# Chosen key blocks of the samples: turned by VectorE in 32x32 blocks and scored in sixteen 32x32 tiles, with the values as a stream of their own

## The chip, the cores and the metric

The kernel runs on one core of a Trainium2 chip, as one launch. The metric is the device time of that launch in microseconds (us). TensorE (PE in the profile; PEld is its weight load), VectorE (DVE), ScalarE (ACT), GpSimd (POOL) and SyncE (SP) each take their own instructions in the order in which they were written, and meet at semaphores. SP issues nearly all transfers.

## What is computed

One inference step of one hybrid layer: a prompt of 256 tokens and a sample group of 8 sequences with 8 new tokens each, and 2048 past tokens a sequence in paged caches. All data are 32-bit floats. Cut to what matters here:

```
u = RMSNorm(x) @ w_in                        # 2048 -> 23664 columns, split among the mixers
y = x + (sigmoid(m_A) * (GDN(u) @ w_branch_a) + sigmoid(m_B) * (NSA(u) @ w_branch_b)) @ w_out
# NSA, for a sample sequence, 16 heads in 4 groups, head dim 128: three attentions are summed
#   compressed keys -> importance -> the chosen blocks of 64 keys (13 best of 30, and 3 always kept)
#   chosen:  s = q @ k.T * 128 ** -0.5 + bias;  p = softmax(s over chosen keys);  o = p @ v
#   window:  the same over the last 512 past tokens
# GDN: a gated delta rule with a state of 128 x 128 a head
```

For the chosen blocks the kernel scores all 2048 past keys of a sequence (16 pages of 128 tokens x 4 groups x 128, 256 KB a page, fetched by page number) and adds a mask m that is very low for a block that was not chosen. Queries of a sequence are 4 groups x 32 rows (4 heads x 8 tokens), so scores and outputs use the 128 partitions as four quarters of 32, one a group.

## The kernel before

The program is written by Python streams (generators). Class `Run` keeps a rough clock of every engine while it writes the program; it always lets that stream take its next step which can start first by this clock. What comes out is a fixed order of instructions on each engine. All compute calls go through the helper at L320 (transfers through L292), so the profile is read by tile names, not by lines.

The backbone is the projection stream: weights are loaded to `wraw` (tiles of 1 MB, three of them), split by ACT into a rounded part `whi` and by DVE (some by POOL) into a rest `wlo` (pieces of 128x512), at most four pieces ahead of TensorE, and multiplied as three matmuls of 320 columns a 128x128 block into `acc` (`acc<-hhi,whi`, `acc<-hlo,whi`, `acc<-hhi,wlo`). It has the lowest claim on TensorE and so fills what other streams leave. Its slabs are queued in stages: until the samples' attention is done, the queue holds only the slabs of queries, keys, values, gates and of 16 heads' z_A, 4752 projection matmuls in all; the slabs of the delta net are queued by code that stands behind `run.go(lambda: done["sample"] == 3)`.

In the samples' part three things come one after the other and overlap: compressed keys (`compressed`, pages `cpg`), window (`window`), chosen blocks (`sample`). `sample` is run twice at the same time (`worker(0)`, `worker(1)`), each for four sequences with ten page tiles `spg` of its own, first the 16 key pages of a sequence and then its 16 value pages. For keys (`scores`, two pages at a time) each page is turned on TensorE by four 128x128 transposes into PSUM (`nt`), copied to SBUF (`kT`, DVE and ACT in turn), and multiplied by the queries:

```
for g in range(4):
    T.transpose(nt[:, g * P:g * P + P], pg[:, g * P:g * P + P], ident)
...
for g in range(4):
    T.matmul(ns[32 * g:32 * g + 32, (p - e.nt + k) * P:(p - e.nt + k + 1) * P], qT(b, g), kT[:, g * P:g * P + P], start=True, stop=True)
```

Each of these score products contracts over 128 rows and fills 32 output rows. Four pages share a bank `ns`, which DVE scales and masks into `xs` (128 x 2112). Then come the 64 new keys, the maximum (DVE), the exponential (ACT), and `weighted`: probabilities `xs` are transposed on TensorE four pages at a time (`nt`), copied (`pT`) and multiplied with the value pages (`op`). The result `o` is turned once more (`tp`) and kept in `obS`, which goes to memory as `d_ob` at the end of all eight.

Behind this stage stands the gated delta net, 16 groups, in which DVE is the busiest engine beside TensorE, and the branch and output products.

Of the kernel before, what the change touches and what calls it, by code (L numbers as in the profile page):

```python
# [21 lines left out]
P = 128  # L22
DM = 2048
NT = 320                 # token columns: 256 of the prompt, then 8 x 8 of the samples
TP = 256
B = 8
# [8 lines left out]
NV = 647                 # distances 519..-127, falling  # L35
NU = 383                 # distances -127..255, rising
WC = 2048                # words a partition of a tile of weights
NRC = 3                  # tiles of weights loaded
NHI = 4                  # pieces of weights split ahead
NPL = 4                  # the first pieces, all split by Pool  # L40
NLP = 4                  # one of so many pieces is split by Pool
CR = -1                  # rank of the compressed keys
OR = -4                  # rank of the moving operand of branch B
NWP = 5                  # pages of the window loaded ahead
SW = ((10, (0, 1, 2, 4)), (10, (3, 5, 6, 7)))  # two streams of chosen blocks: pages loaded ahead, sequences
NM = 3                   # slabs of gates made at the end of the delta net
ZS = (0, 1, 2, 4, 6, 8, 10, 12, 14, 16, 18, 20, 22, 24, 26, 28)  # heads whose z_A are made before the delta net starts


# ---------------------------------------------------------------- constants of the shapes alone  # L50
# [31 lines left out]
def _packs():  # L82
# [48 lines left out]
    tok = np.flatnonzero(i % 32 < 16)                      # of the samples: sequences g and g + 4 at 32 g, their queries 16 behind  # L131
# [26 lines left out]
def bc(ap, dims):  # L158
    """The same memory with other free dimensions [step, count]."""
    return bass.AP(tensor=ap.tensor, offset=ap.offset, ap=[list(ap.ap[0])] + [list(x) for x in dims])  # L160
# [9 lines left out]
class Clock:  # L170
    """A rough clock of every engine, kept while the program is emitted, to order the streams of work by."""
    # from the end of an engine's instruction to the start of one that waits for it
# [4 lines left out]
    def __init__(self):  # L177
        self.t = dict.fromkeys(("pe", "act", "dve", "pool", "sp", "dge", "dma"), 0.0)
        self.parts, self.cut, self.psum = {}, {}, set()          # cut: of a bank: the column that parts it in two
        self.slot = {}                                     # of a tile's name: its place in its pool  # L180
        self.w, self.r = {}, {}                            # of a place: (time, engine) of its last write, read
        self.last = (0.0, "sp")
        self.set, self.lock, self.narrow, self.cold = None, False, False, True

    def key(self, ap):
        n = ap.tensor.name
        k = self.slot.get(n)
        if k is None:                                      # an input or output: nothing waits for it
            return None
# [49 lines left out]
    def table(self, name):  # L239
        """The functions that ACT is loaded with."""  # L240
# [27 lines left out]
class Timed:  # L268
    """An engine whose instructions also move the clock."""
# [4 lines left out]
    def __getattr__(self, op):  # L274
# [9 lines left out]
        def g(*a, **k):  # L284
# [8 lines left out]
            if self.name == "pe":  # L293
# [12 lines left out]
                if self.clock.cold:                        # TensorE at half its speed  # L306
                    ns *= 2
# [16 lines left out]
class Run:  # L324
    """Emits several streams of work, always the one whose next step can start first by the clock.

    A stream yields, before each step, the engine that the step starts on, alone or with the tiles that it waits for
    (alone: it waits for the result of its last step), or a function that is true once the stream may go on."""
# [18 lines left out]
    def _start(self, x):  # L347
# [9 lines left out]
        if e == "exp":                                     # on ACT, with the functions of EXPSET  # L357
# [24 lines left out]
class Next:  # L382
    """The place that the next tile of a tag will have."""
# [12 lines left out]
class Place(Next):  # L396
    """A part of a tile that is written again."""
# [8 lines left out]
class Pool:  # L406
    """A pool of tiles that tells the clock which tiles share a place."""
# [18 lines left out]
def step(ctx: ExitStack, tc: tile.TileContext, I, O):  # L426
# [25 lines left out]
    def newton(y, x, t):  # L452
        """One step of y towards x ** -0.5."""
# [54 lines left out]
    def pieces():  # L508
        """Conditions to wait for, then pieces of weights, in the order of their products."""
# [73 lines left out]
    # ------------------------------------------------------------ normalised input  # L583
# [30 lines left out]
    def gain():  # L614
        """The gain on every partition."""
# [31 lines left out]
    def x_turn(ti, xt, ss, q):  # L647
        """Four columns of tiles of the input, normalised, turned and in two parts."""
# [28 lines left out]
    # ------------------------------------------------------------ tables of the relative bias  # L677
    lastB = tab.tile([P, 520], F32, name="lastB")              # of the last 512 past tokens and the 8 new ones
    winB = tab.tile([P, 8], F32, name="winB")                  # of the first of them, out of the window
# [3 lines left out]
    pB = btab.tile([P, 16, 256], F32, name="pB")               # columns rise with the distance  # L683
# [71 lines left out]
    # ------------------------------------------------------------ native sparse attention  # L755
# [72 lines left out]
    def rstd(pl, pp, tag, src, n, exact, tags=("sq", "rs", "nt")):  # L828
        """(mean of squares over the partitions + eps) ** -0.5 on every partition; a generator."""
# [44 lines left out]
    def prepare():  # L874
        # b, a and the gates by token
# [111 lines left out]
    def prompt():  # L987
        yield lambda: done["names"]
        qp = {}
        for g, tt in ((g, tt) for g in range(4) for tt in range(2)):  # L990
# [8 lines left out]
            # compressed keys, the four heads of the group at once  # L999
# [79 lines left out]
    # ---- samples: compressed keys  # L1079
# [11 lines left out]
    class Feed:  # L1091
        """Tiles loaded ahead of their use, in order."""
# [6 lines left out]
        def load(self):  # L1099
            for r in self.reqs:  # L1100
# [3 lines left out]
                self.out.append(r(t))                      # what is to be written once it is there  # L1104
# [17 lines left out]
    def page(key, b, p):  # L1122
        def f(t):
            k = key[2:], b
            if k not in pnum:                              # the page numbers of a sequence, for its keys and values
                for x in [x for x in pnum if x[0] == k[0] and x[1] % 2 == b % 2 and k[0] == "sel" or x[0] == k[0] == "cmp"]:
                    del pnum[x]
# [99 lines left out]
    def select(h):  # L1227
        """The 13 best of the blocks 1..30 (lower index first among equals); 0, 31 and 32 are always kept."""
# [32 lines left out]
    # ---- samples: window  # L1261
    class Env:
        """Where a stream of attention of the samples keeps its tiles: PSUM tags of sums and transposes, pool and number of others."""
# [17 lines left out]
    def scores(e, b, npg, dst, kS, finish):  # L1281
        """Raw products of the queries of b with npg pages of keys and the 64 new keys."""
# [94 lines left out]
    def add_o(x, g, b):  # L1377
        """Into the sum over the branches."""
# [16 lines left out]
    # ---- samples: chosen blocks  # L1395
    sm = pool(nsa_ctx, "sm")
    obS = sm.tile([P, 16, 64], F32, name="obS")

    def sample(smp, sps, n, bs):
        req = [page(key, b, p) for b in bs for key in ("k_sel", "v_sel") for p in range(16)]  # L1400
        env = Env(sps, "s", "t", 2, smp, 2, "", Feed(smp, "spg", n, req))
        for b in bs:
# [924 lines left out]
```

## Time and profile before

| | |
|---|---|
| time, median of 3 runs | 2684.83 us (2684.65 to 2687.64) |
| profiled execution: span on the core | 2682.3 us; the page gives no other time of it, and the median run lies 2.5 us above this span |
| TensorE busy | 97% of the span |
| DVE, ACT, POOL busy | 63%, 51%, 25% |
| chosen blocks | from about 822 to 1172 us of the span |
| transfers in that stretch | 292 GB/s, 0.86 of the 16 DMA engines' time |

A record of the profile is one hardware instruction. A matmul of 32-bit operands other than the transposes and the projection's (whose operands are rounded parts) shows as two weight loads and two matmuls, two passes. Records overlap on TensorE, since a matmul starts before the one ahead has drained, so what one costs is read from the distance between starts and not from its own length.

### The profile page before, as it was taken

The numbers are of one execution on the slowest core, as the hardware profiler recorded it, in microseconds if no ns is written. First come the engines' busy times: TensorE is split into PE (matmuls) and PEld (weight loads), VectorE is DVE, ScalarE is ACT, GpSimd is POOL, SyncE is SP. The second block draws the span as 40 slices with busy tenths as digits, with TensorE's granted clock in tenths as the row PEclk, the third lists the DMA queues.
The fourth block names the chain that finished last, engine by engine and source line by source line (L and its number), as shares of the span: only waits on it lengthen the run. The fifth ranks groups of instructions, "written<-read, shape, count | busy, mean of one in ns | idle before, by whom it ended". The sixth has DMA issues, their size and how long they took to land.

```text
span 2682.3 us, 58837 instructions
## 1 busy us (share of the span) xinstructions
PE 2612.6 (97%) x22228; PEld 2330.2 (87%) x22228; DVE 1701.1 (63%) x3738; ACT 1358.9 (51%) x3098; POOL 675.2 (25%) x913
## 2 busy tenths in 40 slices
PE   7999999999999999999999999999999999999999
PEld 6898888887888888899889898888888879999999
DVE  5554446555554655445987888888888875455543
ACT  5453443344343333336667666666666555544443
POOL 2000011000000000012454554555545444211111
PEclk9999999999999999999999999999999989999999
DMA  6747776878768898865345455444454355756554
GB/s 198 235 143 254 240 246 214 271 263 281 255 231 307 284 336 286 283 210 179 117 146 163 154 157 177 135 138 147 138 167 156 129 184 185 228 179 193 179 190 133
DMA packets 548671, 543.84 MB, mean 203 GB/s; under 512 B 32482, under 2 KB 452499, under 8 KB 548003
## 3 DMA queue, kind: packets, MB, share of 16 engines
q1 hardware_dynamic: 534308, 493.67, 57.1%
q0 software_dynamic: 14080, 46.41, 5.0%
q8 instruction: 175, 2.87, 0.4%
q14 instruction: 108, 0.88, 0.1%
HBM read 470.31 MB, written 69.67 MB: 201 GB/s over the span
## 4 chain that ended last, share of the span: by engine, by line
PE 86%; DVE 10%; issue 2%; ACT 1%; DMA 0%; POOL 0%; SPq 0%; DVEq 0%; ACTq 0%; POOLq 0%
PE acc L320 61%; PE ps L320 6%; PE nt L320 4%; PE op L320 3%; PE pp L320 3%; PE ns L320 2%; DVE wlo L320 2%; PE tp L320 1%; PE p L320 1%; DVE cv L320 1%; PE sp L320 1%; PE bank L320 1%; DVE at L320 1%; DVE Xd L320 1%; PE ms L320 1%
## 5 line engine op out<-in xcount | busy, mean ns | idle before, releaser
L320 PE MATMUL acc<-hhi,whi 128*128 128x320 f32 (+1 forms) x3472 | 1159.8, 334 | 1.2 <-ACT whi L320 0.8
L320 PE MATMUL acc<-hhi,wlo 128*128 128x320 f32 (+1 forms) x3472 | 1078.6, 311 | 1.1 <-DVE wlo L320 1.1
L320 PE MATMUL acc<-hlo,whi 128*128 128x320 f32 (+1 forms) x3472 | 1077.7, 310 | 0.4 <-DVE hlo L320 0.4
L320 ACT ACTIVATE whi<-wraw 128x512 fp32r<-128x512 f32 (+1 forms) x996 | 626.0, 630 | 866.9 <-PE acc L320 806.0
L320 DVE TENSOR_TENSOR wlo<-wraw,whi 128x512 fp32r<-128x512 f32 x838 | 606.7, 727 | 507.4 <-ACT whi L320 498.0
L320 PEld LDWEIGHTS acc<-hhi,whi 128*128 128x128 f32 (+1 forms) x3472 | 657.6, 189 | 93.4 <-issue 73.7
L320 PEld LDWEIGHTS acc<-hlo,whi 128*128 128x128 f32 (+1 forms) x3472 | 658.7, 190 | 7.6 <-issue 2.4
L320 PEld LDWEIGHTS acc<-hhi,wlo 128*128 128x128 f32 (+1 forms) x3472 | 656.8, 189 | 1.9 <-DVE wlo L320 1.9
L320 POOL TENSOR_TENSOR wlo<-wraw,whi 128x512 fp32r<-128x512 f32 (+1 forms) x158 | 208.8, 1322 | 420.6 <-ACT whi L320 389.3
L320 DVE SCALAR_TENSOR_TENSOR cv<-xp,cw,cv 128x344 f32<-128x344 f32 x192 | 139.6, 728 | 30.7 <-ACT cv L320 28.6
L292 POOL DMA_DIRECT2D d_mz<-raw x48 | 26.4, 550 | 523.8 <-ACT raw L320 489.1
L320 PE MATMUL acc<-oah,whi 128*128 128x320 f32 x512 | 158.2, 309 | 0.0
L320 PE MATMUL acc<-oal,whi 128*128 128x320 f32 x512 | 158.2, 309 | 0.0
L320 PE MATMUL acc<-oah,wlo 128*128 128x320 f32 x512 | 158.2, 309 | 0.0
L320 ACT ACTIVATE kT<-nt 128x512 f32<-128x512 f32 x80 | 47.7, 596 | 101.0 <-PE ns L320 55.2
L320 PEld LDWEIGHTS acc<-oah,whi 128*128 128x128 f32 x512 | 96.1, 188 | 0.0
L320 PEld LDWEIGHTS acc<-oal,whi 128*128 128x128 f32 x512 | 96.1, 188 | 0.0
L320 PEld LDWEIGHTS acc<-oah,wlo 128*128 128x128 f32 x512 | 96.1, 188 | 0.0
L320 DVE COPY kT<-nt 128x512 f32<-128x512 f32 x80 | 55.2, 691 | 63.9 <-PE ns L320 41.3
L320 POOL TENSOR_TENSOR vx<-v,pk_gdn 128x512 fp32r<-128x512 f32 x64 | 68.7, 1073 | 82.1 <-DVE v L320 39.7
L320 PE MATMUL pp<-cpg,Pk 128*32 128x512 f32 x608 | 82.7, 602 | 0.0
L320 POOL TENSOR_TENSOR sS<-sS,ends 128x1024 f32<-128x1024 f32 x32 | 61.8, 1930 | 38.8 <-PE ps L320 38.7
(422 smaller groups left out, 3613.8 us busy)
## 6 DMA issues: line engine op xcount, KB each, us to landing
wraw<-w_in SPq DMA_DIRECT2D x136, 1024.0 KB
wraw<-w_in SPq DMA_DIRECT2D x97, 512.0 KB
cpg<-cache_k_cmp SPq DMA_DIRECT2D x128, 256.0 KB
cpg<-cache_v_cmp SPq DMA_DIRECT2D x128, 256.0 KB
spg<-cache_k_sel SPq DMA_DIRECT2D x128, 256.0 KB
spg<-cache_v_sel SPq DMA_DIRECT2D x128, 256.0 KB
wraw<-w_branch_a SPq DMA_DIRECT2D x32, 1024.0 KB
sS<-state_gdn SPq DMA_DIRECT2D x32, 512.0 KB
```

Of the source, the lines that this page charges most:

```text
L292: return f(*a, **k)
L320: return f(*a, **k)
```

## The change

The two workers become three streams: `quarters`, `keys` and `values`.

- `quarters` copies the queries `qs` once into `q4` by 16 transfers from SBUF to SBUF: quarter d of the head dimension (32 rows) is put on each of the four quarters of the partitions.
- `keys` takes the sequences in order. It has six page tiles `spg` of its own. For each half of a sequence (8 pages) DVE turns every page in blocks of 32x32 straight from `spg` to `kT` (`V.transpose`, one instruction of 128x512 a page; no PSUM, no copy); `kT` holds 8 pages and has one place. Then TensorE multiplies 64 times: for each quarter d of the head dimension, each quarter k of the page's tokens and each group g, one product with 32 rows, 32 output rows and 256 columns (8 pages x 32 tokens); the four d are summed in PSUM, and the four k lie in four different banks `ns`. DVE merges the four banks into `xs` at the end of both halves, so the softmax follows as before. Keys of sequence b start once the values of b-2 are done.
- `values` is `weighted` unchanged, on ten page tiles `spv`, with one PSUM place for the transposed probabilities where there were two for each worker; it follows one sequence behind the keys, and starts once all compressed keys are done.

The page numbers of a sequence are read into registers once for its keys and once for its values, where one reading served both. The diff, cut to its core (the rest takes comments out):

```
-SW = ((10, (0, 1, 2, 4)), (10, (3, 5, 6, 7)))
+NKP, NVP = 6, 10
...
-            k = key[2:], b
+            k = key if key[2:] == "sel" else "cmp", b
...
-    def sample(smp, sps, n, bs):
-        req = [page(key, b, p) for b in bs for key in ("k_sel", "v_sel") for p in range(16)]
-        env = Env(sps, "s", "t", 2, smp, 2, "", Feed(smp, "spg", n, req))
-        for b in bs:
-            yield lambda: done["sel"] > b // 4
...
-            yield from scores(env, b, 16, xs, ksS, fin_s)
...
+    kfeed = Feed(smk, "spg", NKP, [page("k_sel", b, p) for b in range(B) for p in range(16)])
+    ready = []
...
+    def quarters():
...
+        for k in range(4):
+            for d in range(4):
+                yield ("sp", qs)
+                SY.dma_start(q4[32 * k:32 * k + 32, d], qs[32 * d:32 * d + 32])
...
+    def keys():
...
+        for b in range(B):
+            yield lambda: done["sel"] > b // 4 and done["sample"] >= b - 1
...
+            for half in range(2):
+                kT = smk.tile([P, 8, 512], F32, tag="kT", name="kT")
+                for i in range(8):
+                    pg = yield from kfeed.get()
+                    yield ("dve", pg, Place(clock, kT))
+                    V.transpose(kT[:, i], pg)
+                    kfeed.release()
+                yield ("pe", kT, q4, *ns)
+                for d in range(4):
+                    for k, rows in enumerate(quad):
+                        for g in range(4):
+                            T.matmul(ns[k][quad[g], 256 * half:256 * half + 256], q4[rows, d, b, 4 * g:4 * g + 4, :].rearrange("p h t -> p (h t)"),
+                                     kT[rows, :, P * g + 32 * d:P * g + 32 * d + 32], start=d == 0, stop=d == 3)
+            for k in range(4):
+                yield ("dve", ns[k])
+                V.scalar_tensor_tensor(bc(xs[:, 32 * k:], [[P, 16], [1, 32]]), ns[k].rearrange("p (a c) -> p a c", c=32), SCALE,
+                                       bc(m[:, k // 2:], [[2, 16], [0, 32]]), op0=OP.mult, op1=OP.add)
...
+    def values(smv, sps):
+        env = Env(sps, "s", "t", 1, smv, 2, "", Feed(smv, "spv", NVP, [page("v_sel", b, p) for b in range(B) for p in range(16)]))
+        env.nt = 4
...
-    worker(0)
+    run.add(quarters())
+    run.add(keys())
     run.go(lambda: done["cmp"] == B)
     c_ctx.close()
-    worker(1)
-    run.go(lambda: done["sample"] == 3)
+    run.add(values(pool(nsa_ctx, "smv"), pool(nsa_ctx, "sps", 1, PSUM)))
+    run.go(lambda: done["sample"] == B + 1)
     nsa_ctx.close()
```

The order of the written program shows three places. On TensorE (`ns` scores, `nt` transposes, `acc` projections), two pairs of key pages in the seventh of eight sequences before:

```order
L320 MATMUL nt<-pk_const,spg 128x128 x8
L320 MATMUL acc<-hhi,whi 128x320
L320 MATMUL acc<-hlo,whi 128x320
L320 MATMUL acc<-hhi,wlo 128x320
...
L320 MATMUL nt<-pk_const,spg 128x128 x8
L320 MATMUL ns<-kT,qs 32x128 x8
```

and now, eight key pages of a sequence at about the same place (`q_9382` is `q4`):

```order
L320 MATMUL acc<-hhi,wlo 128x320
L320 MATMUL ns<-kT,q_9382 32x256 x64
L320 MATMUL acc<-hhi,whi 128x320
L320 MATMUL acc<-hlo,whi 128x320
L320 MATMUL acc<-hhi,wlo 128x320
...
L320 MATMUL nw<-ksS,qs 32x64 x4
```

The transposes are gone, and the scores stand in bursts of 64. Between the first query block (`mp`) and the end of the chosen blocks the order passes 291 times between projections and other work before, and 136 times now up to the 4752nd projection matmul.

On TensorE at the end of the chosen blocks, before (`op` the products with values, `vsS` the new values):

```order
L320 MATMUL op<-spg,pT 32x128 x8
L320 MATMUL acc<-hhi,whi 128x320
L320 MATMUL acc<-hlo,whi 128x320
L320 MATMUL acc<-hhi,wlo 128x320
L320 MATMUL op<-vsS,pT 32x128 x4
```

and now:

```order
L320 MATMUL acc<-hhi,wlo 128x320
L320 MATMUL ns<-kT,q_9382 32x256 x64
L320 MATMUL nw<-ksS,qs 32x64 x4
L320 MATMUL mp<-selm,pk_nsa 128x32
L320 MATMUL nt<-pk_const,xs 128x128 x8
L320 MATMUL op<-spv,pT 32x128 x16
...
L320 MATMUL op<-vsS,pT 32x128 x4
L320 MATMUL tp<-pk_const,o 128x128
L320 MATMUL acc<-hhi,whi 128x320
```

Before, the last value products stand among projections, and 267 of the 4752 projection matmuls are still to come behind them. Now the 4752nd stands ahead of the second half of the keys of the seventh sequence; from there to the last `tp` no projection matmul is left, and the first of the delta net's comes behind it. From the 4980th projection matmul on, TensorE's order is the same in both.

On SP at the same place, before (`spg` the last value pages, `wraw` weights):

```order
L292 DMA wraw<-w_in 128x8x128 x4
L292 ISA
L292 DMA spg<-cache_v_sel 128x512
...
L292 DMA spg<-cache_v_sel 128x512
L292 DMA d_ob<-obS 128x16x64
L292 DMA wraw<-w_in 128x8x128 x4
```

and now:

```order
L292 ISA
L292 DMA spv<-cache_v_sel 128x512
L292 DMA d_ob<-obS 128x16x64
L292 DMA wraw<-w_in 128x8x128 x4
L292 DMA wraw<-w_in 128x8x256
```

No load of weights stands any more among the last pages: the delta net's first weights are issued behind the store of `obS`.

## Rows read from the trace of the kernel before

**Rows 1.** The page, part 1: busy us, share of the span, instructions.
```profile
PE 2612.6 (97%) x22228; PEld 2330.2 (87%) x22228; DVE 1701.1 (63%) x3738; ACT 1358.9 (51%) x3098; POOL 675.2 (25%) x913
```

**Rows 2.** Windows: stretch, its length, busy us (records), granted clock, DMA share, GB/s.
```profile
822.00:1172.00 350.00, 347.62 (x4060) 292.45 (x4059) 187.76 (x340) 133.31 (x227) 13.01 (x24) 1.00 0.86 292
...
900.00:1000.00 100.00, 99.24 (x1228) 81.71 (x1228) 51.79 (x89) 37.52 (x63) 3.25 (x6) 1.00 0.93 319
```

**Rows 3.** Timeline of TensorE in the stretch: start, length in us, instruction, records.
```profile
960.87 1.04 PE L320 MATMUL nt<-pk_const,spg 128*128 128x128 f32 x8
961.84 0.65 PE L320 MATMUL ns<-kT,qs 128*32 128x128 f32 x16
962.41 1.09 PE L320 MATMUL nt<-pk_const,spg 128*128 128x128 f32 x8
...
966.72 1.04 PE L320 MATMUL nt<-pk_const,spg 128*128 128x128 f32 x8
967.51 0.39 PE L320 MATMUL acc<-hhi,whi 128*128 128x320 f32 x1
...
968.03 0.30 PE L320 MATMUL acc<-hhi,whi 128*128 128x320 f32 x1
...
968.47 0.31 PE L320 MATMUL acc<-hhi,whi 128*128 128x320 f32 x1
```

**Rows 4.** Groups of TensorE's records by tile in 822 to 1172 us.
```profile
L320 PE MATMUL nt<-pk_const,spg 128*128 128x128 f32 x512 | 68.1, 274 | 0.0
L320 PE MATMUL ns<-kT,qs 128*32 128x128 f32 x1024 | 40.7, 278 | 0.0
```

**Rows 5.** Timeline of TensorE: four products side by side, 512 and 32 columns.
```profile
507.23 1.07 PE L320 MATMUL pp<-cpg,Pk 128*32 128x512 f32 x8
508.22 0.41 PE L320 MATMUL acc<-hhi,whi 128*128 128x320 f32 x1
...
1299.34 0.45 PE L320 MATMUL ps<-TTd,A 32*32 32x32 f32 x32
1299.72 0.41 PE L320 MATMUL acc<-hhi,whi 128*128 128x320 f32 x1
```

**Rows 6.** Groups of DVE by shape: busy us, mean ns of one.
```profile
L320 DVE COPY kT<-nt 128x512 f32<-128x512 f32 x80 | 55.2, 691 | 63.9 <-PE ns L320 41.3 <-PE nt L320 22.5
...
L320 DVE STREAM_TRANSPOSE v<-hl 128x256 f32<-128x256 f32 x32 | 14.1, 440 | 0.8
...
L320 DVE STREAM_TRANSPOSE xT<-vS 128x128 f32<-128x128 f32 x32 | 9.7, 304 | 0.4
```

**Rows 7.** Timeline, the last sequence: scores to probabilities, and the end.
```profile
1149.41 0.68 DVE L320 SCALAR_TENSOR_TENSOR xs<-ns,m 128x512 f32<-128x512 f32 x1
...
1150.99 2.35 DVE L320 TENSOR_REDUCE mx<-xs 128x1 f32<-128x2112 f32 x1
...
1153.73 2.04 ACT L320 ACTIVATE xs<-xs,mx 128x2112 f32<-128x2112 f32 x1
...
1157.10 0.60 PE L320 MATMUL nt<-pk_const,xs 128*128 128x128 f32 x4
...
1173.07 0.29 DVE L320 COPY obS<-tp 128x128 f32<-128x128 f32 x1 [0.81 <-PE tp L320]
```

**Rows 8.** SP's timeline behind the stage, and one tile's transfers (d_z).
```profile
1173.39 0.38 SPq L292 DMA_DIRECT2D d_ob<-obS  x1
1174.74 4.51 SPq L292 DMA_DIRECT2D wraw<-w_in  x4
...
L292 POOL DMA_DIRECT2D d_z<-raw x16: 542/542/560, 1053.1 to 1215.9; - x16
...
DMA to landing us min/median/max: 2.0/3.3/5.5
```

**Rows 9.** Split of weights, 1172 to 1200 us: ns min/median/max, first and last start.
```profile
L320 ACT ACTIVATE whi<-wraw x14: 632/632/632, 1173.4 to 1198.4; 128x512 fp32r<-128x512 f32 x14
L320 DVE TENSOR_TENSOR wlo<-wraw,whi x11: 691/692/693, 1174.0 to 1199.0; 128x512 fp32r<-128x512 f32 x11
```

More of the change, by code (lines that the diff above doesn't have):

```diff
@@ L1123, in f @@
         def f(t):
-            k = key[2:], b
+            k = key if key[2:] == "sel" else "cmp", b
             if k not in pnum:
-                for x in [x for x in pnum if x[0] == k[0] and x[1] % 2 == b % 2 and k[0] == "sel" or x[0] == k[0] == "cmp"]:
+                for x in [x for x in pnum if x[0] == k[0]]:
                     del pnum[x]
@@ L1397, in step @@
     obS = sm.tile([P, 16, 64], F32, name="obS")
-    def sample(smp, sps, n, bs):
-        req = [page(key, b, p) for b in bs for key in ("k_sel", "v_sel") for p in range(16)]
-        env = Env(sps, "s", "t", 2, smp, 2, "", Feed(smp, "spg", n, req))
-        for b in bs:
-            yield lambda: done["sel"] > b // 4
+    q4 = sm.tile([P, 4, B, 16, 8], F32, name="q4")
+    kps = pool(nsa_ctx, "kps", 1, PSUM)
+    smk = pool(nsa_ctx, "smk")
+    kfeed = Feed(smk, "spg", NKP, [page("k_sel", b, p) for b in range(B) for p in range(16)])
@@ L1404, in sample @@
+    ready = []
[5 more added lines that the diff above has]
+    def keys():
+        quad = [slice(32 * g, 32 * g + 32) for g in range(4)]
+        for b in range(B):
+            yield lambda: done["sel"] > b // 4 and done["sample"] >= b - 1
             q = 32 * (b % 4)
-            yield ("pe", selm, Next(sps, "s"))
-            mp = sps.tile([P, 512], F32, tag="s", name="mp")
+            yield ("pe", selm, Next(kps, "k0"))
+            mp = kps.tile([P, 512], F32, tag="k0", name="mp")
@@ L1407, in sample @@
             T.matmul(mp[:, :32], N["E"][q:q + 32], selm[q:q + 32, b // 4], start=True, stop=True)
             yield "dve"
-            m = smp.tile([P, 32], F32, tag="m", name="m")
+            m = smk.tile([P, 32], F32, tag="m", name="m")
             V.tensor_scalar(m, mp[:, :32], 1.0, BIG, op0=OP.subtract, op1=OP.mult)
             V.tensor_scalar(m[:, :30], m[:, :30], cmpB[:, 0:1], None, op0=OP.add)
-            xs = smp.tile([P, 2112], F32, tag="xs", name="xs")
-            def fin_s(quad, ns):
-                V.scalar_tensor_tensor(xs[:, quad * P:quad * P + 512].rearrange("p (k c) -> p k c", c=64),
-                                       ns.rearrange("p (k c) -> p k c", c=64), SCALE,
-                                       bc(m[:, quad * 2:quad * 2 + 8], [[1, 8], [0, 64]]), op0=OP.mult, op1=OP.add)
@@ L1419, in sample @@
-            yield from scores(env, b, 16, xs, ksS, fin_s)
+            xs = smk.tile([P, 2112], F32, tag="xs", name="xs", bufs=2)
+            ns = [kps.tile([P, 512], F32, tag=f"k{k}", name="ns") for k in range(4)]
+            for half in range(2):
[11 more added lines that the diff above has]
+                                     kT[rows, :, P * g + 32 * d:P * g + 32 * d + 32], start=d == 0, stop=d == 3)
@@ new lines, in keys @@
+            for k in range(4):
+                yield ("dve", ns[k])
+                V.scalar_tensor_tensor(bc(xs[:, 32 * k:], [[P, 16], [1, 32]]), ns[k].rearrange("p (a c) -> p a c", c=32), SCALE,
+                                       bc(m[:, k // 2:], [[2, 16], [0, 32]]), op0=OP.mult, op1=OP.add)
+            yield ("pe", Next(kps, "k0"))
+            nw = kps.tile([P, 512], F32, tag="k0", name="nw")
+            for g in range(4):
+                T.matmul(nw[quad[g], :64], qT(b, g), ksS[:, g], start=True, stop=True)
@@ L1420, in sample @@
+            yield "dve"
+            V.scalar_tensor_tensor(xs[:, 2048:], nw[:, :64], SCALE, newB[:, 56 - 8 * b:120 - 8 * b], op0=OP.mult, op1=OP.add)
             V.tensor_tensor(xs[:, 1920:2048], xs[:, 1920:2048], lastB[:, 384:512], op=OP.add)
-            mx = smp.tile([P, 3], F32, tag="mx", name="mx")
+            mx = smk.tile([P, 3], F32, tag="mx", name="mx", bufs=2)
             yield from softmax(xs, 2112, b, 1, mx)
+            ready.append((xs, mx))
+    def values(smv, sps):
+        env = Env(sps, "s", "t", 1, smv, 2, "", Feed(smv, "spv", NVP, [page("v_sel", b, p) for b in range(B) for p in range(16)]))
+        env.nt = 4
+        for b in range(B):
+            yield lambda: len(ready) > b
+            xs, mx = ready[b]
+            yield ("pe", xs, Next(sps, "s"))
@@ L1426, in sample @@
             yield ("dve", op, osum)
-            o = smp.tile([P, P], F32, tag="o", name="o")
+            o = smv.tile([P, P], F32, tag="o", name="o")
             V.scalar_tensor_tensor(o, op[:, :P], mx[:, 2:3], osum[:, b], op0=OP.mult, op1=OP.add)
             yield ("pe", clock.last, Next(sps, "t"))
-            tp = sps.tile([P, 512], F32, tag="t", name="tp", bufs=2)
+            tp = sps.tile([P, 512], F32, tag="t", name="tp")
             T.transpose(tp[:, :P], o, ident)
@@ L1433, in sample @@
             V.tensor_copy(obS[:, :, 8 * b:8 * b + 8], tp[:, :P].rearrange("p (h t) -> p h t", t=8))
-        done["sample"] += 1
-        if done["sample"] == 2:
-            yield "sp"
-            SY.dma_start(dram(d_ob, [[NT, P], [P * NT, 16], [1, 64]], TP), obS)
-            done["sample"] = 3
-    def worker(i):
-        run.add(sample(pool(nsa_ctx, f"smp{i}"), pool(nsa_ctx, f"sps{i}", 1, PSUM), *SW[i]))
-    worker(0)
+            done["sample"] = b + 1
+        yield "sp"
+        SY.dma_start(dram(d_ob, [[NT, P], [P * NT, 16], [1, 64]], TP), obS)
+        done["sample"] = B + 1
+    run.add(quarters())
+    run.add(keys())
     run.go(lambda: done["cmp"] == B)
     c_ctx.close()
-    worker(1)
-    run.go(lambda: done["sample"] == 3)
+    run.add(values(pool(nsa_ctx, "smv"), pool(nsa_ctx, "sps", 1, PSUM)))
+    run.go(lambda: done["sample"] == B + 1)
     nsa_ctx.close()
```

## Prediction, made before the changed kernel ran

> **What bounds the kernel now.** I read the page's busy times first: TensorE is busy for 97% of the span [rows 1], and the span of 2682.3 us lies 2.5 us under the median run. A kernel like this is shortened by taking work or waits from TensorE, unless another engine takes its place. Then the windows for the stretch of the chosen blocks: TensorE is busy 347.6 of 350 us at full granted clock, while DVE works 188 us [rows 2]. So here TensorE sets the pace alone; whatever the two streams of attention leave is filled with projection matmuls. But the last column is high too: 292 GB/s and 0.86 of the DMA engines' time over the stretch, 319 GB/s at 0.93 in its fullest 100 us. That is the second bound, close behind. Last the timeline of TensorE, for what the removed instructions cost as distance between starts.
>
> Both programs have the same TensorE order from the 4980th projection matmul on. So the change in time is the change at that point: TensorE work removed and added, plus time in which TensorE now stands idle ahead of it.
>
> **Removed: transposes and scores of the past keys.** Eight transposes (two pages) take 0.97 us from 960.87 to 961.84 when scores follow, and 0.79 us from 966.72 to 967.51 when a projection follows. Sixteen records of scores (two pages, two passes each) take 0.57 us from 961.84 to 962.41 [rows 3]. There are 512 transposes and 1024 score records [rows 4], so 64 such pairs of pages: 64 x (0.79 + 0.57) = 87 us to 64 x (0.97 + 0.57) = 99 us. I take 93 us.
>
> **Removed: changes between kinds of work.** Three projection matmuls take 0.44 us among themselves (968.03 to 968.47), and 0.52 us behind transposes (967.51 to 968.03) [rows 3]. The order changes 291 times between projection and other work before and 136 times after; half of these are returns, so 78 x 0.08 = 6 us go.
>
> **Added: 16 bursts of 64 products.** Each product has two passes of 256 columns, so a burst is 128 records on sixteen tiles (4 quarters of rows by 4 of columns), each tile used for four d. What the trace has of this is four products side by side, each in its own column quarter: four with 512 columns and two passes take 0.99 us (507.23 to 508.22), two waves of 0.50 us; 32 records of 32x32 tiles, on four tiles along the diagonal, take 0.38 us, eight waves of 0.048 us [rows 5]. A line through both gives 0.26 us for a wave of 256 columns. No row has products side by side that share a column quarter and differ in rows. If all sixteen go side by side, a burst is 8 waves, 2.0 us, 33 us in all; if only four do, 32 waves, 8.2 us, 131 us in all. I take 33 us: the rows show four quarters of rows at work at once on the diagonal and four quarters of columns at once with full rows, each row quarter here has its own bank to write to, and the number of streams read from a partition is the four of the 512-column row. The Trainium skill, page "TensorE: Matmul & The Clock Gate", section "Part 3: Packing small matmuls", gives 10.6 times for sixteen tiles in place of 16; as an estimate by it the bursts take about 49 us and the sum below ends at a gain of 2 us instead of 18.
>
> **DVE and ACT.** 64 copies of 0.69 us leave DVE and as many leave ACT. A block transpose takes 304 ns for 128 columns and 440 ns for 256 [rows 6], so 0.71 us for 512 by that line; 128 of them are 91 us (0.88 us each, 113 us, if 512 cost twice 256). With about 22 more weight pieces inside the stage (0.69 us each [rows 9]) DVE goes from 188 to about 250 us, some 70% of the stage: hidden by TensorE's work as long as no transpose is held up. That is a new wait: a transpose waits for a page from memory, and behind it on DVE queue the weight rests `wlo`, for which the projections wait. Four pieces are split ahead, 16 x 0.44 = 7 us of projections. ACT's 64 copies cost nothing either way, since the copies lay beside TensorE's work.
>
> **The end of the stage.** Here the order matters. The projection slabs that may run in this stage end with the 4752nd matmul. Before, the stage ends with 267 of them left. Now the clock that writes the order charges the bursts far more than 2 us (its cost rule puts 135 ns on each of the 64 products, 8.6 us), places more projections beside them, and runs out: the second half of the seventh sequence's keys, its values, the eighth's keys and values come with nothing between. The chain there, from rows: from the last score to the first transposed probability 1149.41 to 1157.10 with one merge, three more merges of 0.68: 9.8 us. Then the eighth sequence's keys on DVE: two halves of 8 x 0.71 and a burst of 2 us, with copies and merges some 18 us, beside the seventh's values. Again 9.8 us. Then the values: five rounds of transposing, 0.69 us of copy and hand-offs (0.2 us each, an estimate), and `o`, `tp`, `obS`, about 10 us; in the trace 1157.10 to 1173.36 with projections between, so 10 to 16 us [rows 7]. Then the delta net's first weights, which no load ahead covers any more: from the copy's end to the first issue 1.4 us, 1.1 us an issue, 3.3 us to land (the median of `d_z`, a smaller transfer) [rows 8], 0.63 and 0.69 us of splitting [rows 9], 7 us. With the first burst 57 us. TensorE's own work in it is in the sums already: three bursts 6 us, and two sets of values, each 17 transposes of 0.11 us and 64 products at eight in 0.57 us, 6.5 us. Idle: 57 - 19 = 38 us. The bounds are 28 us (hand-offs overlapping, weights landing sooner) and 50 us (values at 16 us, half clock after idling).
>
> **Transfers.** The last of the 4752 matmuls is stored at 1215.9 us now [rows 8], 394 us after 822. After the change TensorE could be there after 394 - 93 - 6 + 33 - 19 = 309 us. In the stage before 102 MB move (350 us at 292 GB/s [rows 2]). Afterwards 224 of the 256 pages of 0.262 MB are asked for ahead of that point (118 of keys, 106 of values), 8.4 MB fewer, and 89 blocks of weights of 64 KB more, 5.8 MB, with 2 MB of `q4`: 101 MB, 327 GB/s. The fullest 100 us had 319. At that rate the stage takes 317 us, 8 us more; at 343 GB/s (319 over its share 0.93) nothing; at the mean of the stage before, 292, it takes 346 us, 37 us more. I take 10 us.
>
> **Sum.** -93 - 6 + 33 + 38 + 10 = -18 us, from 2684.8 to 2667 us. A measurement of this kernel tells 0.2%, 5.4 us, from no change.
>
> **Rivals.**
>
> *Pages come late (the other side).* DVE's block transposes wait for pages, `wlo` queues behind, and TensorE waits for weights. For it speak 327 GB/s asked where 319 was the best 100 us, only six key pages ahead, eaten in 4 us of transposes, and one place for `kT`; against it that values have ten pages ahead and that TensorE was idle for 2.4 of the 350 us so far [rows 2]. At 292 GB/s it costs 37 us in place of 10: +9 us, 2694. It decides from 28 us of stalls on, 1.8 us for each of the 16 halves.
>
> *Sixteen tiles do not run side by side.* Four at a time: +98 us on the sum, less the 10 us of stalls and some idle that the longer bursts fill: 2745. Nothing in the trace excludes it; the reasons against are above.
>
> *They do, but each wave takes half as long again.* 16 us more: 2683, no change. The rows of four side by side show nothing of the kind. The skill's 10.6 of 16 named above would be this case.
>
> *More is won.* If transfers hold and the end costs 28 us of idle, the sum is -38: 2647. For it: the fullest 100 us kept 0.93 of the DMA engines' time busy, so 343 GB/s may be had [rows 2]; against it, the end of the chain is counted in rows, and few of its links overlap.
>
> *The change does not do what it says* would need transposes or scores left on TensorE; the order shows none.
>
> **Chances.** The sum as written, with its own range 2652 to 2679: 0.38. More won: 0.18. Pages late: 0.20. Waves half as long again: 0.10. Four at a time: 0.10. That leaves 0.04 for causes behind the stage. Faster by over 0.2%: 0.38 and 0.18 and a little of the late pages, 0.58. Within 0.2%: the slow waves and part of the late pages, 0.13. Slower: 0.29. The range has to leave out no more than 2 in 10: from 2638 (more won, without any stall) to 2710 (late pages at their worst, about 40 us beyond the sum); four at a time lies outside.
>
> **What the profile after would show.** Right: no `nt<-spg`, 128 block transposes of about 0.71 us on DVE, 2048 score records in 16 bursts of about 2 us each; in TensorE's windows a hole of nearly 40 us of idle with no `acc` at the end of the stage, with waits on DVE (`xs`, `kT`, `pT`) and then on the first `whi` or `wlo`. Wrong: bursts of 3 us or 8 us; TensorE idle inside the stage on `wlo` behind a transpose that waits for `spg`; or the end without a hole. Most of the prediction hangs on the bursts and on the end: without the hole the gain would be near 56 us, and with bursts of four there would be none.

## The result, and the profile after

The changed kernel takes 2708.07 us (median of 4 runs, 2705.99 to 2712.97), the kernel before beside it 2684.74 us: a ratio of 1.0089, with a 95% interval of 1.0077 to 1.0101. The prediction was 2667 us, faster. The change costs 23 us where 18 were to be won.

The page's first part, to be held against [rows 1]: TensorE is busy for 34 us less, in a span 22 us longer.

```profile
PE 2578.2 (95%) x22740; PEld 2293.2 (85%) x22740; DVE 1736.6 (64%) x3806; ACT 1321.0 (49%) x3034; POOL 670.0 (25%) x909
```

Where the time went is found by cutting both spans at the same projection matmuls. First the windows of the kernel before, of `acc` alone (columns as in [rows 2]; the first number in brackets counts the matmuls):

```profile
0.00:819.90 819.90, 568.88 (x3354) 500.78 (x3354) 0.00 (x0) 28.98 (x69) 1.00 0.71 236
819.90:1214.60 394.70, 242.32 (x1398) 205.94 (x1399) 0.00 (x0) 12.17 (x29) 1.00 0.85 287
1214.60:1248.05 33.45, 33.45 (x230) 33.34 (x228) 0.00 (x0) 2.36 (x9) 1.00 0.43 138
```

Then the changed kernel, again of `acc` alone:

```profile
0.00:820.30 820.30, 568.79 (x3354) 500.69 (x3354) 0.00 (x0) 28.93 (x69) 1.00 0.71 236
820.30:1151.66 331.36, 223.37 (x1398) 206.25 (x1398) 0.00 (x0) 12.13 (x29) 0.98 0.88 296
1151.66:1225.60 73.94, 0.15 (x2) 0.00 (x0) 0.00 (x0) 0.44 (x1) 0.64 0.52 170
1225.60:1270.56 44.96, 38.78 (x228) 37.30 (x229) 0.00 (x0) 1.93 (x8) 0.84 0.68 208
```

and two of these windows with all instructions:

```profile
820.30:1151.66 331.36, 313.63 (x4148) 269.61 (x4147) 205.08 (x376) 103.40 (x179) 15.87 (x29) 0.98 0.88 296
1151.66:1225.60 73.94, 35.55 (x712) 22.56 (x710) 27.77 (x49) 8.30 (x13) 0.54 (x1) 0.64 0.52 170
```

The same 1398 projection matmuls took 394.7 us with all that stood among them. Now they are through after 331.4 us, and then comes a hole of 74 us without a projection (two records at its edges). The 230 matmuls behind it take 11.5 us longer. So 331.4 + 73.9 + 45.0 = 450.3 us against 394.7 + 33.5 = 428.2: 22.1 us more. From there to the end both need the same (1434.2 before, 1433.6 after).

The hole is work at a clock of 0.64 and waiting. TensorE's longest waits from 820 to 1226 us are these (us, times, longest); before, the two largest in 820 to 1215 us were 1.8 and 0.6 us:

```profile
PE ns L320 <- DVE kT L320: 22.3, 6, 9.4
PE nt L320 <- ACT xs L320: 10.8, 2, 6.4
PE acc L320 <- ACT whi L320: 8.6, 2, 7.1
```

TensorE waits for `kT`, that is for the block transposes. Their row among DVE's groups, in 815 to 1226 us, says why: they take what was predicted (0.70 us), but DVE sat idle 40.2 us ahead of them for key pages.

```profile
L320 DVE STREAM_TRANSPOSE kT<-spg 128x512 f32<-128x512 f32 x128 | 86.7, 697 | 57.8 <-DMA spg<-cache_k_sel 40.2 <-PE ns L320 17.0
```

DVE's timeline at the beginning of the hole shows it page by page: the last pages of the half come one to three microseconds after DVE was ready for them.

```profile
1150.66 0.71 DVE L320 STREAM_TRANSPOSE kT<-spg 128x512 f32<-128x512 f32 x1 [2.65 <-DMA spg<-cache_k_sel]
...
1153.34 0.71 DVE L320 STREAM_TRANSPOSE kT<-spg 128x512 f32<-128x512 f32 x1 [1.18 <-DMA spg<-cache_k_sel]
1155.34 0.71 DVE L320 STREAM_TRANSPOSE kT<-spg 128x512 f32<-128x512 f32 x1 [1.28 <-DMA spg<-cache_k_sel]
1160.47 2.48 DVE L320 SCALAR_TENSOR_TENSOR xs<-ns,m 128x512 f32<-128x512 f32 x4 [4.42 <-PE ns L320]
```

It isn't that the engines of transfer are full all through the hole. In these two windows of it they stand still (columns as above: 10 and 1 GB/s), since SP's next transfer wants a place whose page nobody has read yet (in the first window for `spg`, in the second for `spv`). Between the two, pages are asked for as places come free, and the chain that ended last goes through their landing (start, length in us):

```profile
1160.00:1171.00 11.00, 3.93 (x49) 2.19 (x26) 7.78 (x15) 2.74 (x3) 0.00 (x0) 0.50 0.04 10
1193.50:1208.50 15.00, 7.30 (x152) 4.45 (x151) 5.86 (x11) 2.74 (x3) 0.00 (x0) 0.50 0.00 1
```

```profile
1150.63 4.68 DMA spg<-cache_k_sel
...
1156.11 4.34 PE ns L320 x116
...
1168.09 1.13 PE nt L320 x4
...
1176.15 6.14 DMA spv<-cache_v_sel
...
1187.52 5.03 DMA spg<-cache_k_sel
...
1193.34 4.33 PE ns L320 x116
...
1205.32 1.13 PE nt L320 x4
...
1212.37 4.58 DMA spv<-cache_v_sel
...
1218.62 0.30 DVE obS L320
...
1219.42 5.51 DMA wraw<-w_in
```

Bursts: in TensorE's timeline 64 products go from 1117.92 to 1120.61, 2.69 us at full clock; the prediction had 2.0. The timeline merges the 128 records; in the trace sixteen of them start within 0.11 us, and the next sixteen begin 0.24 us after the first. That is about as long as four alone take (0.22 to 0.24 us, in the run with the loops turned round below), so sixteen tiles do work side by side. Later in the burst the records start one at a time, 17 ns apart, with three pauses of 0.16 to 0.19 us.

```profile
1117.92 2.76 PE L320 MATMUL ns<-kT,q 32*32 32x256 f32 x128 [0.93 <-DVE kT L320]
1120.61 0.42 PE L320 MATMUL acc<-hhi,whi 128*128 128x320 f32 x1
```

### The profile page after: what moved, and what is told of

It is laid out like the page before. It is cut to its first block, busy times and chain, and to the rows that moved or that the text cites. A ratio compares the mean times of both kernels' runs of the same rounds, so it can differ in the third digit from the quotient of the medians.

```text
span 2704.2 us, 59685 instructions
## 1 busy us (share of the span) xinstructions
PE 2578.2 (95%) x22740; PEld 2293.2 (85%) x22740; DVE 1736.6 (64%) x3806; ACT 1321.0 (49%) x3034; POOL 670.0 (25%) x909
## 4 chain that ended last, share of the span: by engine, by line
PE 66%; issue 16%; DVE 11%; DMA 4%; ACT 1%; POOL 1%; SPq 1%; DVEq 0%; POOLq 0%; ACTq 0%
PE acc L320 50%; PE ps L320 6%; DVE wlo L320 2%; PE pp L320 2%; PE ns L320 1%; DMA spv<-cache_v_sel 1%; PE p L320 1%; PE op L320 1%; PE bank L320 1%; DVE cv L320 1%; DMA spg<-cache_k_sel 1%; DVE at L320 1%; DVE Xd L320 1%; PE nt L320 1%; PE tp L320 1%
## 5 line engine op out<-in xcount | busy, mean ns | idle before, releaser
L292 POOL DMA_DIRECT2D d_mz<-raw x48 | 26.5, 552 | 450.3 <-ACT raw L320 418.2
L320 DVE STREAM_TRANSPOSE kT<-spg 128x512 f32<-128x512 f32 x128 | 86.7, 697 | 57.8 <-DMA spg<-cache_k_sel 40.2
L320 PE MATMUL ns<-kT,q 32*32 32x256 f32 x2048 | 50.3, 430 | 23.2 <-DVE kT L320 22.3
```

Of the source, the lines that this page charges most:

```text
L292: return f(*a, **k)
L320: return f(*a, **k)
```

## The experiments

The theory after the result (A with E below): TensorE lost the work it was to lose, and stands idle instead, because a half of a sequence is eight key pages and there are only six places. The seventh and eighth page can be asked for only when the first two have been turned, and these wait for `kT`, which has one place. The keys' chain gets longer by that; the clock that writes the order fills the longer chain with projections, and these are used up before the last keys. Rivals: transfers too slow (B), the bursts (C), pages in general too late (D), the split into two streams by itself, and the overcharge of the bursts in the clock, which the prediction had named as the reason.

**Eight places for key pages, and, apart from it, twelve for value pages.**

```diff
-NKP, NVP = 6, 10
+NKP, NVP = 8, 10
```

> Eight places for key pages in place of six (values keep ten); nothing else is edited, but the clock then writes another order, in which projections last until the last values instead of running out one and a half sequences earlier. Theory A (a half of a sequence is eight pages, six places let DVE wait for two of them in each half, this stretches the keys' chain and leaves the end without projections): the idle tail of 55 us shrinks to 15 or 20 us, stalls inside the stage stay near 15 us: 2655 to 2675 us. Theory B (the transfers themselves are too slow, 300 GB/s for the stage): the tail goes but the same time comes back as stalls inside the stage: 2690 to 2710. Theory C (the bursts are what costs): no change, 2708.

Measured: 2666.55 us, ratio to before 0.9935 (0.9913 to 0.9957). Theory A holds. In the written order 43 to 45 blocks of projections lie between the `tp` of one sequence and of the next (third to seventh) where it was 54 to 59 (second to sixth), and the supply lasts to the last values. The windows of the stage:

```profile
813.34:1171.80 358.46, 338.96 (x4821) 290.60 (x4823) 230.08 (x422) 110.03 (x188) 15.72 (x29) 0.97 0.91 303
1171.80:1181.87 10.07, 2.23 (x43) 0.88 (x42) 0.64 (x2) 1.28 (x4) 0.54 (x1) 0.68 0.61 172
1181.87:1228.70 46.83, 42.04 (x251) 40.91 (x252) 23.39 (x44) 18.37 (x42) 10.40 (x19) 0.85 0.65 201
```

The hole of 74 us is one of 10. DVE's wait for key pages, in its group of transposes, is 16.0 us instead of 40.2, and TensorE's wait for `kT`, the longest in the changed kernel, is 0.4 us:

```profile
L320 DVE STREAM_TRANSPOSE kT<-spg 128x512 f32<-128x512 f32 x128 | 85.8, 695 | 30.6 <-DMA spg<-cache_k_sel 16.0 <-PE ns L320 14.6
```

```profile
PE ns L320 <- DVE kT L320: 0.4, 1, 0.4
```

```diff
-NKP, NVP = 6, 10
+NKP, NVP = 6, 12
```

> Twelve places for value pages in place of ten, keys keep six. Theory A (the keys' places): little, 2700 to 2710 us, since the order still runs out of projections ahead of the last keys. Theory D (any page asked for earlier helps): a gain of 10 us or more, below 2698.

Measured: 2705.5 us, 1.0084 (1.0057 to 1.0110). More places for values do nothing that can be measured; it is the keys' two places that count, and D falls.

**More projections for the same stage.** `NM` slabs are kept back for the end of the delta net.

```diff
-NM = 3
+NM = 0
```

> After, with three more projection slabs (96 blocks, 288 matmuls, 42 us of TensorE) queued in this stage; they are taken from the end of the delta net, where they were queued before. Theory E (the loss is TensorE idling for lack of projections at the end of the stage): the tail's idle falls by about 40 us and the time to 2665 to 2675, if the delta net does not need these slabs. Rival: the delta net loses its cover and idles as much more: 2700 to 2710.

Measured: 2673.21 us, 0.9947 (0.9931 to 0.9964): 35 us below the changed kernel, with the same six places. Theory E holds. The last projections now stand up to 1212 us and the part without any lasts 18 us:

```profile
1212.20:1230.10 17.90, 8.16 (x155) 4.92 (x153) 2.03 (x4) 2.56 (x6) 0.54 (x1) 0.80 0.61 180
```

**Small key pages, same order.**

```diff
...
+            if key == "k_sel":
+                clock.dma("sp", 4 * 512 * P, t, src)
+                SY.eng.dma_start(t[:, :32], src[:, :32])
+            else:
+                SY.dma_start(t, src)
...
-                    V.transpose(kT[:, i], pg)
+                    V.transpose(kT[:, i], bc(pg[:, :32], [[0, 16], [1, 32]]))
```

> After in the same order, but a key page is loaded only in its first 32 of 512 columns, and DVE turns these 32 columns sixteen times (left out: the other columns, so the scores are others). 31 MB of transfers go. Theory B and the late pages (DVE and TensorE wait for key pages because the transfers are too slow): stalls inside the stage fall from 18 to about 3 us and the tail by 15 to 25 us, 2665 to 2680 us. Theory A in its strict form (what counts is the order, already written, with no projections at the end): inside the stage 10 to 15 us less, the tail only 5 to 10 us less, 2683 to 2695.

The clock that writes the order is charged for the whole page, so the order is that of the changed kernel.

Measured: 2691.63 us, 1.0020 (1.0007 to 1.0032). The stage moves 217 GB/s in place of 296 and still needs nearly as long, and the hole is as good as unchanged, 71 us where it was 74:

```profile
815.67:1142.06 326.39, 313.93 (x4148) 271.87 (x4147) 205.12 (x376) 103.82 (x179) 15.91 (x29) 0.97 0.71 217
1142.06:1213.34 71.28, 33.71 (x711) 21.66 (x710) 26.95 (x48) 8.35 (x13) 0.54 (x1) 0.68 0.41 117
```

So B falls as the main cause: in the traces, the bytes of the key pages are worth 5.0 us inside the stage and 2.7 us in the hole. By the medians it is 16 us; 4.6 us of the difference between the two traces lies ahead of the stage, where both programs are the same (this stretch ends between 813 and 820 us in the traces of these kernels), and the rest I can't place. Small pages come late too: DVE still sits idle 28.3 us for them, in place of 40.2, and the three that the chain goes through in the hole and just ahead of it land 3.6 to 4.2 us after their issue, though each has only 16 KB. For these waits it counts more when a page can be asked for than how many bytes it has.

**Eight places and one slab more**, by its median the best of these kernels (`NKP` 8, `NM` 2):

> Eight places for key pages, and one more projection slab (32 blocks, 14 us of TensorE) queued in this stage. Theory A and E together: with eight places the profile still shows 7.2 us without work ahead of the delta net's first product, 6 us of further gaps behind it, and a clock below full there; the slab's 14 us stand in part of that: 5 to 12 us below the kernel with eight places alone, 2654 to 2662 us. Rival: what it fills here is missing at the end of the delta net, 2666 us.

Measured: 2662.19 us, 0.9921 (0.9904 to 0.9939). TensorE's timeline at the last `tp` now has projections on both sides of it, where the kernel with eight places alone waits 7 us for weights:

```profile
1180.82 0.30 PE L320 MATMUL acc<-hhi,whi 128*128 128x320 f32 x1
...
1181.26 0.27 PE L320 MATMUL tp<-pk_const,o 128*128 128x128 f32 x1
1181.29 0.39 PE L320 MATMUL acc<-hhi,whi 128*128 128x320 f32 x1
```

The intervals of this kernel and of the one without the slab overlap; that the slab itself wins 4 us is not settled.

**The split alone.** `keys` calls `scores` as before (TensorE transposes, copies, two pages at a time), `quarters` is gone, all else as after.

```diff
...
+    kenv = Env(kps, "k0", "kt", 2, smk, 2, "", kfeed)
...
+            yield from scores(kenv, b, 16, xs, ksS, fin_s)
```

> Keys and values as two streams one sequence apart, with six and ten pages, but keys turned on TensorE and copied as before (two pages at a time, full 128-row scores): the split without the transposes of DVE. If six places hurt only because DVE takes pages in halves of eight (theory A), the order keeps its projections to the end and the time is that of before within 8 us: 2677 to 2693. If the split by itself stretches the chain (values can't start until the last key), it is slower than before by 15 us or more, 2700 to 2720.

Measured: 2686.42 us, 1.0006 (0.9994 to 1.0017): the time of before. TensorE is as full as it was (the window of the stage's 1398 projection matmuls), with six places and a reader that takes two pages at a time. The split by itself costs nothing that can be measured.

```profile
817.15:1200.70 383.55, 380.42 (x4346) 336.29 (x4346) 199.96 (x360) 148.18 (x256) 15.99 (x30) 1.00 0.85 283
```

**The loops of a burst turned round.**

```diff
-                for d in range(4):
-                    for k, rows in enumerate(quad):
+                for k, rows in enumerate(quad):
+                    for d in range(4):
```

> After with the loops of a burst turned round: for one quarter k of the rows all four d come after one another, so that only four products (one for each g) are on free tiles at a time. If the sixteen tiles of after really work side by side (a burst of 2.7 us is eight waves of some 0.21 us and the loads of the weights), a burst takes 32 waves now, 6.9 us or more, 4.2 us more each; 13 of the 16 bursts stand in a full TensorE: 2708 and 55 us, less where it was idle anyway, 2740 to 2775. If the order of the products doesn't matter: 2708.

Measured: 2730.15 us, 1.0168 (1.0140 to 1.0195), 0.8% or 21 us above the changed kernel. A burst takes 4.80 us (1076.32 to 1081.12):

```profile
1076.32 4.86 PE L320 MATMUL ns<-kT,q 32*32 32x256 f32 x128
1081.12 1.08 PE L320 MATMUL op<-spv,pT 128*32 128x128 f32 x32
```

The direction is as expected, the size half of it. With only four tiles offered at a time the burst isn't 6.9 us but 4.8, 0.15 us for each of its 32 waves of four records. The records show how: the first four waves start 0.22 to 0.24 us apart, but through most of the rest two waves start within 0.08 us, and the next two 0.22 us after them. So for most of the burst a wave of four isn't alone at work.

**More projections in the kernel before.** The same `NM = 0` there:

> The kernel before, with the same three slabs (42 us of TensorE) queued in the stage of the chosen blocks and taken from the end of the delta net. TensorE is full in that stage before, so by theory E nothing is to be filled: the same time within 6 us, 2679 to 2691. Rival (the slabs are simply better placed here, whatever the stage): 15 us or more faster, as it was for the changed kernel.

Measured: 2685.51 us, 1.0008 (0.9997 to 1.0018). Moving these slabs is worth nothing where TensorE is full, so what they won above was the hole.

**The measured charge for a burst.**

```diff
-ns = max(n * 1.67, 107) if m > 32 else max(n / 2.1 + 13, 34)
+ns = 42 if kk == 32 and n == 256 else max(n * 1.67, 107) if m > 32 else max(n / 2.1 + 13, 34)
```

> After (six places for keys, no more fill), but the clock that writes the order charges one 32x32 product of 256 columns 42 ns, the measured 2.7 us a burst, in place of 135 ns. The prediction had put the lack of projections at the end down to that overcharge. If so, the projections now last longer and the time falls by 15 us or more, to 2693 or less. Theory A (the keys' chain with six places sets the pace also by the clock): the order now runs out one sequence earlier still, and the time rises, 2710 to 2735.

Measured: 2713.76 us, 1.0108 (1.0093 to 1.0124). My reason for the hole was wrong: the time doesn't fall. The interval overlaps that of the changed kernel (1.0077 to 1.0101), so whether the time rises isn't settled; but with the right charge the projections run out earlier (at the fifth sequence's `tp` 4713 of the 4752 projection matmuls are through, where it was 4548), and the hole is 106 us:

```profile
1122.96:1228.60 105.64, 55.53 (x1131) 35.45 (x1130) 45.37 (x81) 11.95 (x18) 0.54 (x1) 0.64 0.60 196
```

**All three together** (`NKP` 8, the charge, `NM` 0):

> Eight places for key pages, the measured charge for a burst, and three more slabs in this stage (42 us of TensorE): the order puts 96 blocks more among the last two sequences and ends with 17 blocks between the last keys and the last values. Theories A and E: TensorE is filled to the end of the stage, the best of these kernels, 2645 to 2660 us. Rival (transfers: the slabs bring 6.3 MB more into a stage whose engines of transfer are at 0.97 in its fullest stretch with eight places): no better than with eight places alone, 2660 to 2672.

Measured: 2671.19 us, 0.9950 (0.9937 to 0.9964): a miss. The interval overlaps that of eight places alone, so nothing is won over it. The time lies in the rival's range, but its cause, full engines of transfer, doesn't show (0.90 to 0.92 of the engines' time from 822 to 1172 us, where eight places alone reach 0.97). The part without projections is back, 23.6 us with 10.3 of work, and what follows it takes 1444.0 us, where eight places alone need 1478.3 with three slabs, 42.0 us of TensorE, more to do: 1444.0 + 42.0 - 1478.3 = 7.7 us more. I put them down to the delta net's lack of the slabs; that is not shown, since taking the same slabs from it cost the kernel before nothing that can be measured.

```profile
1201.80:1225.40 23.60, 10.27 (x154) 6.58 (x154) 4.19 (x8) 4.59 (x8) 0.54 (x1) 0.70 0.47 136
1225.40:2669.40 1444.00, 1383.58 (x11797) 1289.73 (x11797) 1046.65 (x2305) 835.09 (x2054) 582.59 (x768) 0.98 0.53 163
```

## Why the prediction was wrong

*TensorE's own work* held but for one term. Expected were -93 - 6 + 33 = -66 us. Before, TensorE was busy for 392 of 394.7 us (2.4 of 350 idle [rows 2]); now for 313.6, and in the hole for what would be some 21 us at full clock (the prediction's 19 and 2 for three longer bursts, an estimate; the 35.6 us of its row ran at a clock of 0.64). That is 57 us less. The 9 us that are missing are about what the bursts cost more, 16 x 2.69 = 43 us in place of 33; some of it may be the clock, 0.98 in that window. Sixteen tiles do go side by side, so that four at a time is out. The rival of slower waves had 3.0 us a burst; the truth lies between. The Trainium skill ("TensorE: Matmul & The Clock Gate", section "Part 3: Packing small matmuls") had 10.6 times for sixteen tiles, by which the 16 bursts were estimated at 49 us; the trace has 43.

*The hole: the step of the sum that failed most.* The prediction found its place (from the second half of the seventh sequence's keys to the delta net) and counted its chain as 57 us, of which 38 idle. It took 74, of which 53 idle at the same reckoning. The pages were costed as always there, and the bursts at full clock. Link by link, from the starts in the chain above: 4.5 us pass before the first burst, which waits for the seventh sequence's last key pages (nothing was counted); the burst takes 4.3 us (2); from there to the first transposed probability it is 7.6 us, and 7.7 for the eighth sequence (9.8 each); the eighth's keys take 29.6 us (18); its values 13.6 (10), with 4.6 us for value pages; the first weights 6.7 (7). So the excess lies where the chain goes through pages and through bursts at half clock (4.3 us each). (The measured idle time, 74 us less the 35.6 that the work took, is the predicted 38 us; that is chance, since the chain and the work in it were both longer.)

*The reason that failed* is the one given for the hole: "the clock that writes the order charges the bursts far more than 2 us [...], places more projections beside them, and runs out". With the charge mended the projections ran out earlier. Projections fill what other streams leave in that clock, so a burst that is charged less leaves more room for them; that reading of it was not tested by itself. The projections run out because the keys' chain is longer than TensorE's work beside it, and what makes it longer is six places for halves of eight pages: with two places more the hole goes from 74 to 10 us. The prediction spoke of "only six key pages ahead" and of "one place for `kT`", but under a rival, and priced them as slow transfers, 37 us in place of 10; it never compared six with the eight that a half needs.

*Restart.* The "delta net's first weights" were put at 7 us; the wait was 7.06 us. But the next matmuls run at half clock (0.50 granted from 1225.6 to 1233 us), 0.27 us each (three in 0.80, 1227.47 to 1228.27) where three took 0.44 [rows 3], and TensorE waits 0.8 and 2.4 us for constants that are loaded behind the stage, as its timeline shows. The stretch behind the hole takes 45.0 us in place of 33.5: 11.5 us that were not in the sum.

```profile
1225.64 0.64 PE L320 MATMUL acc<-hhi,whi 128*128 128x320 f32 x1 [7.06 <-ACT whi L320]
...
1227.47 0.47 PE L320 MATMUL acc<-hhi,whi 128*128 128x320 f32 x1
...
1228.27 0.47 PE L320 MATMUL acc<-hhi,whi 128*128 128x320 f32 x1
...
1233.26 0.66 PE L320 MATMUL bank<-pk_const,c 64*128 64x64 f32 x4 [0.79 <-DMA al<-gdn_dt_bias]
1236.32 0.68 PE L320 MATMUL bank<-bag,pk_gini 64*128 64x64 f32 x2 [2.41 <-DMA pk_gini<-c_gini]
```

*Transfers.* 10 us of stalls were taken. TensorE's idle time up to the hole is 331.4 - 313.6 = 17.7 us, about 15 more than before. The rival of late pages had the sign (2694 us, 9 over; it was 23) and the first link, DVE waiting for pages. But it took slow transfers, 292 GB/s, for the cause and weights for what TensorE would lack; with a sixteenth of the key bytes the hole stays, and what TensorE waits for is `kT`.

Together: -57 of work, 15 of stalls, 53 idle in the hole and 11.5 of restart make +22.5, where the cut spans show +22.1. Against the terms as predicted (-66, 10, 38, 0) that is 9 + 5 + 15 + 11.5 = 40.5 us, and 2708 - 2667 = 41 were missed. That eight places measure 2666.6 us, the predicted time, is chance: there the hole is 10 us long, and the prediction had 57.

What stays open: whether the six places cost by the order that was written for them or by waits on the chip. An order written for six with eight real places was not tried; the small pages, which keep the order and leave the hole at 71 us, speak for the order. Two more rivals stand untested: a second place for `kT`, and six places with halves cut to four pages.

## What to carry to other kernels

Work taken from the engine that sets the pace is won only if it finds other work at that place; look first how much is left in the queue that fills it, and what the chain beside it takes. When a reader changes from two pages at a time to eight, compare the places for its pages with eight; here two more 256 KB pages turned a loss of 0.9% into a gain of 0.65%. If a planner's model writes the order, a mended cost need not make the order better (here the hole grew from 74 to 106 us); test the reason before trusting it.

## What the runs showed of the hardware that was not expected

- Sixteen 32x32 tiles at four row and four column quarters: 64 fp32 products of 256 columns in 2.69 us, 42 ns a product, when sixteen consecutive products fall on different tiles; 4.80 us, when only four consecutive ones do and the next four add to the same sums.
- DVE turns 128x512 floats in 32x32 blocks in 0.70 us, as long as a copy out of PSUM of that size [rows 6], here from SBUF.
- The granted clock was 0.50, the lower of the two levels (1.2 of 2.4 GHz), in both stretches of the hole shown above (TensorE busy 3.9 of 11 and 7.3 of 15 us), and the first blocks of projections behind the hole were still multiplied at 0.80 us a block, 1227.47 to 1232.00, where one took 0.44 [rows 3].
- A key page of 16 KB took 3.6 to 4.2 us from issue to landing in the chain, one of 256 KB 4.7 and 5.0 us.
